# A small DRAM-to-DRAM copy issued ahead of the first loads of a rotary-embedding kernel

## The chip, the cores and the metric

The kernel runs on one core of a Trainium2 chip. The metric is the device time of one execution in microseconds (us). Several executions are timed, always beside runs of the kernel before on the same chip, and the median is given.

## The reference

```python
# x: (8, 8, 1024, 64) float32, scale = 0.5
angles = np.outer(positions * scale, freqs)          # 1024 x 32
cos, sin = np.cos(angles), np.sin(angles)
out_first  = x_first * cos - x_second * sin          # halves of the last axis
out_second = x_first * sin + x_second * cos
```

The kernel must read 16.8 MB and write 16.8 MB.

## The kernel before

x is cut into eight tiles of 128 x 4096. Tile 0 is loaded as float32 by SyncE (X0f); tiles 1 to 7 are loaded by GpSimd, cast to float16 on the way. Two small loads on ScalarE's queue bring the positions (8 KB) and the frequencies (128 B):

```python
X0f = xin.tile([P, N], FP32, name="X0f")
nc.sync.dma_start(out=X0f, in_=xv[0])

pos_i64 = consts.tile([HP, K], positions.dtype)
nc.scalar.dma_start(out=pos_i64, in_=positions.rearrange("(q k) -> q k", k=K))
freq_row = consts.tile([1, half], FP32)
nc.scalar.dma_start(out=freq_row, in_=freqs[None, :])
# ... loads of X[1] to X[7] on gpsimd ...
# two small matmuls spread frequencies and positions over the partitions,
# VectorE makes the angles (y, m, r, ra), ScalarE their sine and cosine
```

Then follow eight rounds of four VectorE instructions, a cast to float32 on ScalarE and a 2 MB store:

```python
for u in (1, 0, *range(2, NU)):
    # ps = X*sin; X = X*cos; X[first] -= ps[second]; X[second] += ps[first]   (VectorE)
    OUT = xout.tile([P, N], FP32, tag="O")
    pin(nc.scalar.copy(out=OUT, in_=X[u].rearrange("p k h j -> p (k h j)")))
    nc.sync.dma_start(out=ov[u], in_=OUT)
```

## Time and profile before

| what | value |
|---|---|
| time, median of 3 runs | 85.48 us (85.28 to 85.62) |
| span of the profiled execution | 83.9 us |
| VectorE busy | 62.6 us, 75% |
| ScalarE busy | 37.4 us, 45% |
| DMA engines | busy in nearly every slice from about 4 us on |
| bytes read and written in HBM | 16.79 and 16.78 MB |

The page gives the share of busy time of each engine, a strip of 40 slices, and the chain of work that ended last. VectorE's 75% and the DMA engines' full strip are both near a limit, so the page alone doesn't say which sets the end; the prediction takes it from the first packets of the last store. "Landing" below is the moment at which a transfer's completion semaphore has its last count. A transfer is moved in packets; what one queue has given to one DMA engine, in order, is its ring on that engine. The "head" is the part of the kernel up to the landing of the two small loads.

### The profile page before, as it was taken

How to read it: one execution, taken by the hardware profiler on the slowest of the kernel's cores; microseconds unless marked ns; L12 is line 12 of the kernel's file. 1: busy time of each engine (PE TensorE's matmuls, PEld its weight loads, DVE VectorE, ACT ScalarE, POOL GpSimd, SP SyncE). 2: the span in 40 equal slices, each digit the busy share in tenths (PEclk: the TensorE clock that was granted, in tenths of full speed). 3: DMA queues.
4: the chain of work that ended last, by engine and by line, in shares of the span. 5: the costliest groups of instructions: out<-in, count | busy, mean ns of one | idle time of the engine just before them, and what ended most of it. 6: DMA issues, size and time to landing. Idle time of an engine off the chain costs nothing.

```text
span 83.9 us, 151 instructions
## 1 busy us (share of the span) xinstructions
PE 1.1 (1%) x4; PEld 0.9 (1%) x4; DVE 62.6 (75%) x40; ACT 37.4 (45%) x12; POOL 4.5 (5%) x13
## 2 busy tenths in 40 slices
PE   0002300000000000000000000000000000000000
PEld 0002200000000000000000000000000000000000
DVE  0010699889999999999999999999999999600000
ACT  1400000799749309608905921950880591294000
POOL 5960000000000000000000000000000000000000
DMA  3599999999999999999999999999999999998890
GB/s 78 207 402 328 289 207 219 215 211 223 203 230 203 231 191 238 313 336 305 313 348 324 313 313 277 426 438 438 438 430 414 445 414 430 438 430 375 375 500 0
DMA packets 2338, 26.22 MB, mean 313 GB/s; under 512 B 274, under 2 KB 290, under 8 KB 290
## 3 DMA queue, kind: packets, MB, share of 16 engines
q1 hardware_dynamic: 1296, 18.87, 53.6%
q0 software_dynamic: 1008, 7.34, 42.7%
q10 hardware_dynamic: 34, 0.01, 0.2%
HBM read 16.79 MB, written 16.78 MB: 400 GB/s over the span
## 4 chain that ended last, share of the span: by engine, by line
DVE 72%; DMA 8%; ACT 7%; DVEq 1%; PE 1%; issue 1%; ACTq 1%
DVE X L136 22%; DVE ps L135 21%; DVE X L137 12%; DVE X L140 9%; DMA freq_row<-in_freqs_dram 8%; ACT OUT L144 4%; DVE r L116 3%; DVE y L107 3%; ACT sinT L120 2%; DVE m L114 1%; DVEq L176 1%; PE cfreq L92 1%; PE pos_ps L100 1%; ACTq L64 0%; DVE posf L104 0%
## 5 line engine op out<-in xcount | busy, mean ns | idle before, releaser
L144 ACT CAST OUT<-X 128x4096 f32<-128x4096 f16 x8 | 28.8, 3605 | 25.0 <-DVE X L140 25.0
L135 DVE TENSOR_TENSOR ps<-X,sinT 128x4096 f16<-128x4096 f16 x8 | 18.3, 2284 | 0.7 <-ACT sinT L120 0.7
L136 DVE TENSOR_TENSOR X<-X,cosT 128x4096 f16<-128x4096 f16 x8 | 18.3, 2292 | 0.3
L137 DVE TENSOR_TENSOR X<-X,ps 128x2048 f16<-128x2048 f16 x8 | 9.8, 1224 | 0.3
L140 DVE TENSOR_TENSOR X<-ps,X 128x2048 f16<-128x2048 f16 x8 | 9.7, 1217 | 0.0
L120 ACT ACTIVATE sinT<-r 128x2048 f16<-128x2048 f32 x1 | 1.9, 1910 | 12.2 <-DVE r L116 12.2
L71 POOL DMA_DIRECT2D X<-in_x_dram x7 | 3.9, 567 | 0.8 <-POOLq L162 0.8
L127 ACT CAST X<-X0f 128x4096 f16<-128x4096 f32 x1 | 3.6, 3587 | 0.0
L104 DVE COPY posf<-pos_ps 128x64 f32<-128x64 f32 x1 | 0.2, 225 | 4.0 <-PE pos_ps L100 4.0
L95 DVE CAST pos_row<-pos_i 16x64 f32<-16x64 int32 x1 | 0.2, 241 | 3.9 <-DMA pos_i<-in_positions_dram 3.9
L116 DVE SCALAR_TENSOR_TENSOR r<-m,y 128x2048 f32<-128x2048 f32 x1 | 2.3, 2292 | 0.0
L107 DVE TENSOR_TENSOR y<-posf,cfreq 128x2048 f32<-128x2048 f32 x1 | 2.3, 2286 | 0.0
L120 ACT ACT_TABLE_LOAD x1 | 1.3, 1283 | 1.7 <-issue 1.7
L126 ACT ACTIVATE cosT<-ra,quarter 128x2048 f16<-128x2048 f32 x1 | 2.0, 1985 | 0.0
L114 DVE TENSOR_SCALAR m<-y 128x2048 f32<-128x2048 f32 x1 | 1.2, 1227 | 0.0
L122 DVE TENSOR_SCALAR ra<-r 128x2048 int32<-128x2048 int32 x1 | 1.2, 1226 | 0.0
L88 DVE MEMSET coef<- 1x128 f32 x1 | 0.2, 165 | 0.8 <-PEq L162 0.8
L92 PE MATMUL cfreq<-freq_row,coef 1*128 1x32 f32 x2 | 0.6, 392 | 8.0 <-DMA freq_row<-in_freqs_dram 8.0
L100 PE MATMUL pos_ps<-pos_row,sel 16*128 16x64 f32 x2 | 0.7, 432 | 0.0
L92 PEld LDWEIGHTS cfreq<-freq_row,coef 1*128 1x128 f32 x2 | 0.5, 308 | 7.9 <-issue 7.9
L100 PEld LDWEIGHTS pos_ps<-pos_row,sel 16*128 16x128 f32 x2 | 0.5, 328 | 0.0
L77 POOL TENSOR_SCALAR_AFFINE_SELECT sel<-sel 16x128 f32<-16x128 f32 x1 | 0.3, 332 | 0.1
(6 smaller groups left out, 0.7 us busy)
## 6 DMA issues: line engine op xcount, KB each, us to landing
out_dram<-OUT SPq DMA_DIRECT2D x8, 2048.0 KB, 14.3
X<-in_x_dram POOLq DMA_DIRECT2D x7, 1024.0 KB, 24.5
X0f<-in_x_dram SPq DMA_DIRECT2D x1, 2048.0 KB, 10.2
pos_i<-in_positions_dram ACTq DMA_DIRECT2D x1, 8.0 KB, 4.1
freq_row<-in_freqs_dram ACTq DMA_DIRECT2D x1, 0.1 KB
```

The lines of the kernel that those rows point to most:

```text
L71: nc.gpsimd.dma_start(out=X[u].rearrange("p k h j -> p (k h j)"), in_=xv[u])
L100: nc.tensor.matmul(out=pos_ps, lhsT=sel.rearrange("q a b -> q (a b)"), rhs=pos_row, start=True, stop=True)
L107: pin(nc.vector.tensor_tensor(out=y, in0=posf.unsqueeze(2).broadcast_to((P, K, half)), in1=cfreq.unsqueeze(1).broadcast_to((P, K, half)), ...
L114: pin(nc.vector.tensor_scalar(out=m, in0=y, scalar1=_MAGIC, scalar2=None, op0=ALU.add))
L116: pin(nc.vector.scalar_tensor_tensor(out=r, in0=m, scalar=_MAGIC, in1=y, op0=ALU.subtract, op1=ALU.subtract))
L120: pin(nc.scalar.activation(out=sinT, in_=r, func=AF.Sin, bias=0.0, scale=-_TWO_PI_DN))
L127: pin(nc.scalar.copy(out=X[0].rearrange("p k h j -> p (k h j)"), in_=X0f))
L135: pin(nc.vector.tensor_tensor(out=ps, in0=X[u], in1=sin_b, op=ALU.mult))
L136: pin(nc.vector.tensor_tensor(out=X[u], in0=X[u], in1=cos_b, op=ALU.mult))
L137: pin(nc.vector.tensor_tensor(out=X[u][:, :, 0, :], in0=X[u][:, :, 0, :], in1=ps[:, :, 1, :], op=ALU.subtract))
L140: pin(nc.vector.tensor_tensor(out=X[u][:, :, 1, :], in0=ps[:, :, 0, :], in1=X[u][:, :, 1, :], op=ALU.add))
L144: pin(nc.scalar.copy(out=OUT, in_=X[u].rearrange("p k h j -> p (k h j)")))
```

## The change

One DMA is added, first on ScalarE's queue: sixteen rows of 128 floats (512 B), 1 MiB apart, are copied from x to out within DRAM. The result stores later overwrite all of them, so the result doesn't change. The question is what a transfer of 8 KB costs in a kernel that moves 33.6 MB.

```diff
     X0f = xin.tile([P, N], FP32, name="X0f")
     nc.sync.dma_start(out=X0f, in_=xv[0])
+
+
+    R = 16
+    xr = x.rearrange("b h s d -> (b h s d)").rearrange("(r n) -> r n", r=R)
+    outr = out.rearrange("b h s d -> (b h s d)").rearrange("(r n) -> r n", r=R)
+    nc.scalar.dma_start(out=outr[:, 0:128], in_=xr[:, 0:128])
 
     pos_i64 = consts.tile([HP, K], positions.dtype)
     nc.scalar.dma_start(out=pos_i64, in_=positions.rearrange("(q k) -> q k", k=K))
```

## The prediction

> **What bounds the kernel now.** I read the page's strip of the DMA engines first, then the chain that ended last, then the waits, then busy time by stage, and last the packet records that the trace keeps for every DMA packet (queue, start, duration, size).
>
> From the page, the busy share of the 16 DMA engines in 40 slices of 2.1 us:
>
> ```profile
> DMA  3599999999999999999999999999999999998890
> ```
>
> The engines are full from about 4 us to the end. The kernel reads 16.79 MB and writes 16.78 MB, and the last stores complete 4.9 us apart (63.00, 67.88, 72.72, 77.56 us in the semaphore updates): that is 2 MB in 4.87 us. Eight loads and eight stores at that pace are 78 us. So DMA alone nearly makes the 83.9 us, whatever the page's "DVE 72%" of the chain says.
>
> The chain, in order of time (start us, us, what):
>
> ```profile
> 0.74 0.41 ACTq L64
> 1.16 0.03 issue
> 1.19 6.64 DMA freq_row<-in_freqs_dram
> 7.82 0.14 issue
> 7.96 0.60 PE cfreq L92 x2
> 8.56 0.49 PE pos_ps L100 x2
> ...
> 15.24 1.92 ACT sinT L120
> 17.16 0.02 issue
> 17.19 2.30 DVE ps L135
> ...
> 71.59 1.15 DVEq L176
> 72.73 0.03 ACTq L144
> 72.76 0.04 issue
> 72.80 3.60 ACT OUT L144
> ```
>
> The reader is to see that the chain begins with the 128 bytes of freq_row, issued at 1.19 us and landed at 7.82 us, and that from there to 76.4 us no piece waits: angles, sine, eight rounds on VectorE (6.92 us each), the last cast. The waits say the same:
>
> ```profile
> PE cfreq L92 <- DMA freq_row<-in_freqs_dram: 8.0, 1, 8.0
> PEld cfreq L92 <- issue: 7.9, 1, 7.9
> DVE posf L104 <- PE pos_ps L100: 4.0, 1, 4.0
> DVE pos_row L95 <- DMA pos_i<-in_positions_dram: 3.9, 1, 3.9
> DVE ps L135 <- ACT sinT L120: 0.7, 1, 0.7
> ```
>
> VectorE never waits for an x tile; positions land 3 us before freq_row and don't count. Now the end, by stage (window: us, busy of PE, PEld, DVE, ACT, POOL, clock, DMA share, GB/s):
>
> ```profile
> 54.00:77.20 23.20, 0.00 (x0) 0.00 (x0) 18.52 (x12) 12.46 (x4) 0.00 (x0) 1.00 0.99 422
> 77.20:84.00 6.80, 0.00 (x0) 0.00 (x0) 0.00 (x0) 0.00 (x0) 0.00 (x0) 1.00 0.73 308
> ```
>
> The two bounds meet at 77.2 us. The DMA engines finish the last-but-one store between 76.74 and 77.22 us (its completion packets). The last store is issued at 76.45 us and its first packets start at 77.27 to 77.41 us on all engines alike, the ones free since 76.74 and the one free at 77.22. So it is its issue that they waited for (0.82 us from issue to first packet), not the engines. The compute chain therefore ends last, by 0.05 us against the last engine. That has a one-sided consequence: a later head of the chain moves the end by its full amount; an earlier head would gain next to nothing.
>
> **What the Trainium skill says.** Three places in its page "DMA: Bandwidth & Descriptors" bear on the change.
> (1) "Queues, rings and completion order": each DMA engine round-robins between the queues with work, a packet at a time, and works off one queue's ring in order. The trace agrees. I followed each engine's packets by end and start. Leaving out two engines' muddled first microseconds, all go: x (X0f, 16 KB, 0.62 us), pos data (25 ns when undisturbed), x, pos completion, x, x, x, then x and gpsimd-load packets alternately. The engine that carries freq_row has: pos data 3.34, pos completion 4.39, three x packets at 4.39, 5.01, 5.62, freq data 6.25, a load packet 6.25, x 6.86, freq completion 7.48, landed 7.82.
> (2) "Why a DMA increments its semaphore by 16 and not by 1": the slowest dimension sets the number of engines, the lowest-numbered ones being used. By that the new copy (16 rows on both sides) and positions use all 16 and freq_row one. The trace agrees for the old two: 16 packets for positions, one for freq_row, and freq_row's semaphore moves at 1.79 and 7.82 us.
> (3) "Latency and other measured facts" puts HBM access at 0.2 us on average and 2 us under high load. The trace has more in a full queue: the first store, issued at 27.93 us among loads, has its first packets at 31.94 to 33.3 us, 4.0 us and more, against 0.82 us for the last store on idle engines. So a packet entering a busy engine stands behind some 3.2 us or more of packets already taken, about five of 0.62 us. That also explains freq_row: three x packets got in between it and positions because it came a little later.
>
> **The change, part by part.** Nothing is removed and no compute instruction is added or moved: the instruction orders of both kernels on TensorE, VectorE, GpSimd and SyncE are the same. ScalarE's queue gets one DMA ahead of positions and freq_row.
> - Bytes: 16 rows of 512 B, one data and one completion packet on each engine: about 25 + 9 ns per engine by positions' packets of the same size. Nothing in 80 us.
> - ScalarE issue: positions took 0.41 us from 0.74. The copy takes that place, so positions go from about 1.16 and freq_row from about 1.6 us, some 0.45 us later. ScalarE itself is not needed before 15.24 us.
> - The dependency that the overwriting makes: the built kernel's first store has an extra wait for the copy's semaphore. That store is issued at 27.93 us, the copy should land by some 5 to 6 us. Worth 0. The semaphores shift by one among the eight; each reused one belongs to a transfer long landed. Worth 0.
> - Ring order: this is the cost. The copy's packets take positions' early places (data about 3.5, completion about 4.3 us). Positions are now issued when freq_row was (1.16 against 1.19 us), so they should get its place: data near 6.2 us. From there each further packet of ScalarE's queue waits a full round, one x packet and one load packet, 1.24 us (6.245 to 7.480 in the records). On the freq engine: pos data 6.25, pos completion 7.48, freq data 8.72, freq completion 9.95, landed 10.3 us. X0f's completion packets come at about 10 to 10.5 us, so the round keeps its length that long.
> - Sum: freq_row lands at about 10.3 instead of 7.82 us: +2.5 us, the whole of it on the path, for the chain is tight behind it and the last store has 0.05 us of slack. 85.48 + 2.5 = 87.95 us. Because the sizes below 2.5 have more weight than those above, I put the prediction at 87.7.
>
> **The rivals.**
> - One place fewer: positions are issued 0.1 us sooner than freq_row was (their issue is shorter, 0.41 against 0.53 us), and may get in before the three x packets. Then pos data would come about 5.0, completion 5.6 to 6.2, freq data 7.5, completion 8.7: +1.24 us, 86.7 us, 1.5%, within 2%. For it: the exact filling of the engines in the first 2 us is not visible. Against: freq_row missed those places by three packets, not by one.
> - The issue alone counts, +0.45 us, 85.9 us, or the copy takes a first-use cost on itself (positions' first packets took up to 0.44 us against 0.025) and the others keep their times. Against: freq_row's 6.6 us lie in waiting behind packets, and the ring is in order.
> - Worse: a DRAM-to-DRAM copy may hold the ring longer than a load, since its completion waits for a write to DRAM, or positions and freq_row each find the engines full anew (1.9 us between positions' completion and freq data). Each lost place is 1.24 us: +3.7 us, 89.2 us. No DRAM-to-DRAM transfer is in this trace to say.
> - The copy delays the first store, or is hidden since DMA is the bound anyway: both give 85.5. The first is excluded by 20 us of slack; the second by the 0.05 us of slack in the last store. DMA being full in the middle doesn't help, for its backlog is used up exactly when the last store is issued.
> - Faster: nothing is removed, and before the last store there is no slack to win on the DMA side. 2%.
>
> **Range and chances.** Delay 0 to 0.6 us: 12%; about 1.2: 20%; 1.7 to 2.8: 53%; more: 15%. The line of 2% is 1.71 us. Slower by over 2%: 0.67; within: 0.31; faster: 0.02. Range for 8 in 10: 86.4 to 88.8 us.
>
> **What would show it.** In the changed profile: the DMA piece of the chain that ends with freq_row's landing near 10.3 us (right) or below 9.2 (wrong); positions landing near 7.9; every later piece of the chain with its old length and shifted by the same amount; no wait of the first store on anything but its cast; the last store's landing again about 6.2 us after its issue. The prediction is wrong if freq_row lands at its old time, if the copy lands later than positions, if VectorE shows a new wait later on, or if the end moves by less than freq_row does.

## The result, and the profile after

| kernel | time, median | range | ratio, 95% interval |
|---|---|---|---|
| before | 85.38 us | 85.12 to 85.62 (4 runs) | |
| changed | 88.97 us | 88.83 to 89.06 (4 runs) | 1.0419 (1.0383 to 1.0455) |

A ratio is the mean time of one kernel's runs over that of the other's runs of the same rounds, so it is not quite the ratio of the medians. The change costs 3.6 us. The direction was predicted, the size was not: 87.7 us was said, and 88.97 lies just above the range (86.4 to 88.8).

The start of the chain that ended last, changed kernel (start us, us, what):

```profile
0.75 0.61 ACTq L67
1.37 0.03 issue
1.40 0.60 ACTq L70
2.00 0.04 issue
2.04 9.28 DMA freq_row<-in_freqs_dram
11.31 0.14 issue
11.45 0.60 PE cfreq L98 x2
...
18.73 1.92 ACT sinT L126
...
76.28 3.60 ACT OUT L150
```

L67 is the copy, L70 the load of positions. The frequencies land at 11.31 us instead of 7.82, 3.49 us later. From there on every piece has its old length: the sine starts at 18.73 instead of 15.24 us (+3.49), the last cast at 76.28 instead of 72.80 (+3.48). The whole loss is made before 11.4 us.

The DMA issues (KB each, median us from issue to landing), positions in the kernel before, then the copy and positions in the changed one:

```profile
pos_i<-in_positions_dram ACTq DMA_DIRECT2D x1, 8.0 KB, 4.1
...
out_dram<-in_x_dram ACTq DMA_DIRECT2D x1, 8.0 KB, 7.3
pos_i<-in_positions_dram ACTq DMA_DIRECT2D x1, 8.0 KB, 9.1
```

An 8 KB copy took 7.3 us to land, and positions, which took 4.1 us before, took 9.1. The Trainium skill, "Perfetto Trace Analysis", "DMA Instruction — HWDGE (DVE, Sync)", warns that a DMA instruction that looks fast in the profile may still be waiting for its execution. The runs agree: in the kernel before, freq_row was issued in 0.53 us and landed 6.6 us after its issue began.

The end, by stage (window, us, then busy time and count of PE, PEld, DVE, ACT and POOL, clock, DMA share, GB/s):

```profile
54.00:78.50 24.50, 0.00 (x0) 0.00 (x0) 21.99 (x14) 13.04 (x4) 0.00 (x0) 1.00 0.91 387
78.50:80.70 2.20, 0.00 (x0) 0.00 (x0) 0.00 (x0) 1.38 (x1) 0.00 (x0) 1.00 0.00 0
80.70:87.40 6.70, 0.00 (x0) 0.00 (x0) 0.00 (x0) 0.00 (x0) 0.00 (x0) 1.00 0.74 313
```

Before the last store the DMA engines now stand still (share 0.00), where in the kernel before that store met them just as they came free. In the packet records they end the store ahead of it at 78.89 us and begin the last at 80.74. So in the kernel before the two bounds met, and in the changed one the compute chain alone sets the end.

Why were the frequencies 3.49 us late? These are the packets of the engine that carries freq_row, from the packet records (start in us; x is a 16 KB packet of X0f, load one of GpSimd's loads; data and done are the data and completion packets of a ScalarE DMA):

```
before:  pos data 3.34, x, pos done 4.39, x, x, x 5.62, freq data 6.25, load, x, freq done 7.48
changed: x, x, x, x, x 5.37, copy data 6.00, load, x, copy done 7.25, load, x,
         pos data 8.48, load, x, pos done 9.73, load, freq data 10.34, load, freq done 10.97
```

The copy came behind X0f's first five packets on each engine (80 of X0f's packets start ahead of it, five for each of 16). Call the place behind X0f's first packet (data near 3.4 us) the early one and the place behind its first five (near 6 us) the late one: the copy did not take the early place of positions; it took the late place of freq_row.

### The profile page after: what moved, and what is told of

The parts are those of the page before. It is cut to its first block, busy times and chain, and to the rows that moved or that the text cites.

```text
span 87.3 us, 153 instructions
## 1 busy us (share of the span) xinstructions
PE 1.1 (1%) x4; PEld 0.9 (1%) x4; DVE 62.5 (72%) x40; ACT 37.4 (43%) x12; POOL 4.5 (5%) x13
## 4 chain that ended last, share of the span: by engine, by line
DVE 69%; DMA 11%; ACT 6%; ACTq 1%; DVEq 1%; PE 1%; issue 1%
DVE X L142 21%; DVE ps L141 20%; DVE X L143 11%; DMA freq_row<-in_freqs_dram 11%; DVE X L146 9%; ACT OUT L150 4%; DVE r L122 3%; DVE y L113 3%; ACT sinT L126 2%; DVE m L120 1%; DVEq L182 1%; ACTq L67 1%; ACTq L70 1%; PE cfreq L98 1%; PE pos_ps L106 1%
## 5 line engine op out<-in xcount | busy, mean ns | idle before, releaser
L98 PE MATMUL cfreq<-freq_row,coef 1*128 1x32 f32 x2 | 0.6, 390 | 11.4 <-DMA freq_row<-in_freqs_dram 11.4
L98 PEld LDWEIGHTS cfreq<-freq_row,coef 1*128 1x128 f32 x2 | 0.5, 304 | 11.4 <-DVE pos_row L101 11.4
```

## The experiments

The theory after the result: (a) each engine takes ScalarE's packets in order, one per round, and a round lasts 1.24 us while both X0f and GpSimd's loads have packets waiting; (b) who is issued at once with X0f comes behind its first packet, who is issued some tenths later comes behind the first five (c2 below found four); (c) the copy is late by its own slower issue and loses that race, and everything behind it moves along. The main rivals: a DRAM-to-DRAM copy costs by itself wherever it stands; the distance of its rows costs; the number of DMAs alone costs; VectorE's chain is not what the end follows. Eleven kernels were run, all with correct results.

| run | what is on ScalarE's queue, or changed | freq_row landed, us | time, median us | ratio to before |
|---|---|---|---|---|
| before | pos, freq | 7.82 | 85.4 | |
| changed | copy, pos, freq | 11.31 | 88.97 | 1.042 |
| a1_copy_last | pos, freq, copy | 7.61 | 85.34 | 0.999 |
| a2_copy_second | pos, copy, freq | 9.95 | 87.71 | 1.027 |
| a3_load_first | small load, pos, freq | 10.04 | 87.62 | 1.026 |
| a4_contig | copy of adjacent rows, pos, freq | 10.61 | 88.95 | 1.040 |
| b2_sp_behind | pos, freq; copy on SyncE behind X0f | 7.47 | 85.30 | 1.000 |
| c2_late_pos | pos 0.29 us later, freq | 8.71 | 86.55 | 1.014 |
| c1_sp_first | copy, pos, freq; X0f 0.43 us later | 10.29 | 88.15 | 1.033 |
| b4_freq_sp_first | pos; freq on SyncE ahead of X0f | 1.94 | 85.73 | 1.005 |
| d1_two_copies | copy, copy, pos, freq | 12.42 | 90.25 | 1.056 |
| b1_one_row | copy of 16 x 32 B, pos, freq | 11.24 | 88.98 | 1.041 |
| b3_freq_first | freq, pos | 2.45 (pos 7.95) | 85.59 | 1.003 |

A landing is that of the profiled execution, a time is the median of all, so the two need not match within a row: the profiled execution of the kernel before took 85.65 us. Within the profiled executions, the time less the landing of freq_row is 77.74 to 77.84 us for the kernel before and for all eight kernels with a later freq_row. So the delay of freq_row passed to the end whole, in each of them.

### a1_copy_last: the copy behind the two loads

```diff
-    nc.scalar.dma_start(out=outr[:, 0:128], in_=xr[:, 0:128])   # first
     (loads of pos_i64 and freq_row on nc.scalar)
+    nc.scalar.dma_start(out=outr[:, 0:128], in_=xr[:, 0:128])
```

> The same copy, but third on ScalarE's queue, behind positions and freq_row. Theory (what costs is only that the copy stands ahead of the two small loads in one ring): positions land near 4.9 us and freq_row near 7.8 us as in the kernel before, and the time is 85.4 us, within 0.5% of it. Rival (the copy costs wherever it stands, by its write to DRAM or by the first store's extra wait for it): the time stays near 89 us, or at least over 87.

Measured: 85.34 us, ratio 0.9993 (0.9976 to 1.0009). Positions landed at 4.82 and freq_row at 7.61 us. The copy with all its bytes, its write to DRAM and the extra wait of the first store costs nothing when nothing needed soon stands behind it. The rival that it costs wherever it stands falls.

### b2_sp_behind: the copy on the other queue

```diff
-    nc.scalar.dma_start(out=outr[:, 0:128], in_=xr[:, 0:128])
+    nc.sync.dma_start(out=outr[:, 0:128], in_=xr[:, 0:128])     # behind X0f
```

> The same copy issued from SyncE, behind X0f, and ScalarE's queue as in the kernel before. Theory (the cost is the copy's place ahead of the small loads in ScalarE's ring): positions and freq_row keep their places, freq_row lands near 7.7 us, 85.4 us within 0.5%. Rival (the copy's DRAM-to-DRAM descriptors or bytes disturb the engines wherever they come from): freq_row over 9 us, 86.5 us or more.

Measured: 85.30 us, ratio 0.9997 (0.9984 to 1.001). freq_row landed at 7.47 us; the copy itself at 12.07, 10.9 us after its issue began. Nothing waits for it before the first store.

### a2_copy_second: the copy between them

```diff
     (load of pos_i64 on nc.scalar)
+    nc.scalar.dma_start(out=outr[:, 0:128], in_=xr[:, 0:128])
     (load of freq_row on nc.scalar)
```

> The copy between positions and freq_row. Theory (places in the ring, a round of 1.24 us for each packet once the engines are full): positions keep their early place and land near 4.9 us, the copy takes the place that freq_row had (data near 6.2, completion near 7.5 us), freq_row's packets follow at 8.7 and 9.95 us and land near 10.3 us, so +2.5 us, 87.9 us. Rival (a DRAM-to-DRAM copy holds the ring by itself for longer than a load of its size would): freq_row lands at 11 us or later, 88.7 us or more.

Measured: 87.71 us, ratio 1.0268 (1.0239 to 1.0298). On the engine of freq_row: copy data 5.92, copy done 7.17, freq data 8.40, freq done 9.64, landed 9.95 us. These are steps of 1.25, 1.23 and 1.24 us. A copy ahead of one load costs two rounds, no more; a copy doesn't hold the ring for longer than a load would. This kernel costs about what had been predicted for the change (87.7 us), because here something does hold the early place.

### a3_load_first: an ordinary load in the copy's place

```diff
-    nc.scalar.dma_start(out=outr[:, 0:128], in_=xr[:, 0:128])
+    rows = consts.tile([R, 128], FP32)
+    nc.scalar.dma_start(out=rows, in_=xr[:, 0:128])
```

> In place of the copy a load of the same sixteen rows of 512 B into an SBUF tile that nothing reads, first on ScalarE's queue. Theory A (a DRAM-to-DRAM copy is slower to issue, 0.61 us on ScalarE against 0.41 us for positions, and therefore comes behind the first five X0f packets): the load is issued in about 0.41 us, takes the early place between X0f's first and second packet, positions take freq_row's old place, freq_row lands near 10.3 us, 87.9 us. Theory B (it does not matter what the first DMA is; three DMAs on this queue lose the early place in any case): data of the first load near 5.7 us, freq_row lands near 11.3 us, 88.9 us.

Measured: 87.62 us, ratio 1.026 (1.0232 to 1.0289). The issues on ScalarE (start us, us):

```profile
0.74 0.41 ACTq L68 DMA_DIRECT2D rows<-in_x_dram  x1
1.18 0.44 ACTq L71 DMA_DIRECT2D pos_i<-in_positions_dram  x1
1.64 0.53 ACTq L73 DMA_DIRECT2D freq_row<-in_freqs_dram  x1
```

The same issues of the changed kernel, where the copy is L67:

```profile
0.75 0.61 ACTq L67 DMA_DIRECT2D out_dram<-in_x_dram  x1
1.40 0.60 ACTq L70 DMA_DIRECT2D pos_i<-in_positions_dram  x1
2.04 0.62 ACTq L72 DMA_DIRECT2D freq_row<-in_freqs_dram  x1
```

The load is issued in 0.41 us, the copy in 0.61, and what follows the copy is slower too. The load took the early place (it landed at 4.70 us), positions the late one (landed 7.81), and freq_row landed at 10.04 us. So the outcome is theory A's: three DMAs need not lose the early place; the first of them lost it because it was a copy. That the slower issue is the whole reason is not shown by this run (see what stays open). This load does just what the prediction said that the copy would do.

### c2_late_pos: no copy, but positions a little later

```diff
+    tc.keep_in_program_order(nc.vector.memset(pos_i64.bitcast(I32), 0))
     (load of pos_i64 on nc.scalar, now waits for the memset; freq_row behind it)
```

> No copy at all: the kernel before, with VectorE clearing the positions tile first, so that the issue of positions on ScalarE waits for it and ends some 0.2 to 0.4 us later (near 1.4 to 1.5 instead of 1.15 us); freq_row stays behind it. Theory (the early place is a race: what is issued some tenths later comes behind X0f's first five packets on each engine): positions' data near 5.8 us and landing near 7.5 us, freq_row one or two rounds of 1.24 us later than before (its data at 7 to 8.5, landing near 9 to 10.3 us), so +1.2 to +2.5 us, 86.6 to 87.9 us, from a delay of a few tenths. Rival (it is something in the DRAM-to-DRAM copy itself, not its issue time, that cost the early place): positions stay early or shift by the same tenths, freq_row lands by 8.3 us, 85.4 to 85.9 us.

Measured: 86.55 us, ratio 1.0142 (1.0127 to 1.0156). The issues on ScalarE (start us, us):

```profile
1.03 0.38 ACTq L65 DMA_DIRECT2D pos_i<-in_positions_dram  x1
1.44 0.53 ACTq L67 DMA_DIRECT2D freq_row<-in_freqs_dram  x1
```

The issue of positions began at 1.03 instead of 0.74 us, 0.29 later. Positions' data then came at 4.76 to 5.83 us, behind four X0f packets instead of one, and landed at 6.78 instead of 4.85; freq_row landed at 8.71. A delay of 0.29 us cost 1.93 us at positions and 1.2 us of time. That the places behind X0f's first packets are a race of tenths is shown, without any copy. The expectation was a little off in its numbers: positions lost three places, not four, and landed 0.7 us sooner than expected.

### c1_sp_first: the copy as in the change, X0f a little later

```diff
+    rows = consts.tile([16, 128], FP32)
+    nc.sync.dma_start(out=rows, in_=<16 x 512 B of tile 0 of x>)
     nc.sync.dma_start(out=X0f, in_=xv[0])
```

> The changed kernel, with a small load of 16 x 512 B (its tile is not read) on SyncE ahead of X0f, so that X0f is issued some 0.4 us later while the copy stays at 0.75 us. Theory (race between the copy's issue and X0f's first packets): the copy gets an early place, its data before 4 us; positions may get one too or take the place near 6 us; freq_row lands at 10.5 us or sooner, 1 us or more better than the changed kernel less the 0.4 us that X0f starts later, 87 to 88.3 us. Rival (a DRAM-to-DRAM copy needs over 4 us by itself before its data moves): its data at 5.7 us or later as before, freq_row at 11.3 us or later, 88.9 us or more.

Measured: 88.15 us, ratio 1.033 (1.0315 to 1.0345). The issues to landing (KB each, us):

```profile
out_dram<-in_x_dram ACTq DMA_DIRECT2D x1, 8.0 KB, 2.4
rows<-in_x_dram SPq DMA_DIRECT2D x1, 8.0 KB, 1.7
pos_i<-in_positions_dram ACTq DMA_DIRECT2D x1, 8.0 KB, 6.8
```

With X0f issued at 1.18 instead of 0.75 us, the same copy landed after 2.4 us instead of 7.3; its data moved before 2.8 us. So it was mostly the five packets ahead of it, and not a slowness of the copy, that made 7.3 us. Positions' data came at 6.21 to 6.58 us, and freq_row landed at 10.29 us, 1.02 us sooner than in the change; that X0f's packets start later (2.25 instead of 1.75 us) takes part of the gain. The copy also needed more time than the load of the same size that SyncE issued at the same moment: 2.4 against 1.7 us to landing, and its first data came at 2.13 against 1.76 us.

### a4_contig and b1_one_row: neither the rows nor the bytes

```diff
-    nc.scalar.dma_start(out=outr[:, 0:128], in_=xr[:, 0:128])
+    # a4: 16 rows of 512 B side by side, outr[0, 0:2048] <- xr[0, 0:2048]
+    # b1: outr[0:1, 0:128] <- xr[0:1, 0:128], which the build cuts into 16 x 32 B
```

> The copy first as in the change, but sixteen rows that lie side by side in DRAM (8 KB in one piece, still cut into 16 rows of 512 B on both sides). Theory (the spacing of the rows, 1 MiB, is not what makes the copy late): its data packets start near 5.7 us again and freq_row lands near 11.3 us, 88.9 us. Rival (the spacing of 1 MiB slows its reads or writes): the copy gets the early place, freq_row lands near 10.3 us or sooner, 87.9 us or less.

> The copy first, but of 512 B in one piece, which is cut into sixteen pieces of 32 B. Theory (it is packets and places that count, not bytes): as the changed kernel, freq_row near 11.3 us, 88.9 us within 0.6. Rival (the bytes or the sixteen distant rows count): clearly nearer to the kernel before, under 87.9 us.

Measured: a4 88.95 us, ratio 1.0398 (1.0358 to 1.0439); b1 88.98 us, ratio 1.0408 (1.0392 to 1.0425). Neither the 1 MiB between the rows nor fifteen sixteenths of the bytes matter. The profiled execution of a4 was the fastest of its four (88.36 us) and has freq_row at 10.61 us, sooner than the 11.3 expected. In it, on the engine of freq_row, one packet and not two lay between the copy's data (about 5.90 us) and its completion (6.53, against 7.25 in the changed kernel), and all that stands behind came 0.72 us sooner, freq_row's data at 9.62; the place can thus vary by a packet from one execution to the next. The medians don't differ.

### d1_two_copies: a second copy

```diff
     nc.scalar.dma_start(out=outr[:, 0:128], in_=xr[:, 0:128])
+    nc.scalar.dma_start(out=outr[:, 128:256], in_=xr[:, 128:256])
```

> Two copies first (the second of the next 128 columns of the same rows), then positions and freq_row. Theory (two rounds for each DMA ahead in the ring, 1.24 us a round while X0f's packets last, about 0.62 us when they are gone at some 10.3 us): copy data 5.7 and completion 7.0, second copy 8.2 and 9.5, positions near 10.3 to 10.8 and 10.9 to 11.4, freq_row near 11.6 and 12.2 us, landed near 12.5 us, that is +1.3 us on the changed kernel, about 90.2 us. Rival 1 (each copy has a fixed cost of its own, 3.5 us like the first): 92.4 us. Rival 2 (a fixed 2.5 us for each): 91.4 us. Rival 3 (the first copy alone costs): 89 us.

Measured: 90.25 us, ratio 1.0555 (1.0537 to 1.0573); freq_row landed at 12.42 us. The second copy costs 1.3 us, not 3.5 and not 2.5. When positions' turn comes, X0f's data packets have gone, and on the engine of freq_row the steps shrink from 1.25 us (second copy: data 8.37, done 9.62) to 0.61 (positions' data 10.23, then 10.87, 11.48, 12.09). This separates the number of rounds from their length. On ScalarE the issue of positions took 0.91 us here.

### b3_freq_first: the two loads exchanged

```diff
-    (load of pos_i64, then load of freq_row)
+    (load of freq_row, then load of pos_i64)
```

> No copy: freq_row first and positions second on ScalarE's queue. Theory (one early place, whoever is first gets it): freq_row lands before 5 us, positions take the later place, their data near 5.9 and landing near 7.5 to 8 us, and the head is as long as before: 85.4 us within 1%. Rival (freq_row is late because it is a one-engine transfer of 128 B): freq_row is still late with positions early or late, and the time 86 us or more.

Measured: 85.59 us, ratio 1.0031 (1.0012 to 1.0051). From the waits (who waited for whom: us in total, times, longest):

```profile
DVE pos_row L100 <- DMA pos_i<-in_positions_dram: 7.0, 1, 7.0
...
PE cfreq L97 <- DMA freq_row<-in_freqs_dram: 2.6, 1, 2.6
```

freq_row, whose 128 B took until 7.82 us before, landed at 2.45 us when issued first, and positions now come late (landed 7.95). One early place is to be had, and both loads are needed, so the exchange gains nothing.

### b4_freq_sp_first: an earlier head

```diff
+    nc.sync.dma_start(out=freq_row, in_=freqs[None, :])   # ahead of X0f
     nc.sync.dma_start(out=X0f, in_=xv[0])
     (load of pos_i64 alone on nc.scalar)
```

> No copy: freq_row is issued from SyncE ahead of X0f, positions alone on ScalarE. This tests the step that an earlier head gains next to nothing, since the DMA engines are the other bound. Theory: freq_row lands before 4 us, positions near 4.9 us, VectorE starts on the angles some 3 us earlier and ends 3 us earlier, but the last store waits in the queue for the stores ahead of it (over 9 us from its issue to landing instead of 6.2), and the time is 85.0 to 85.9 us, within 1% of the kernel before. Rival (the chain on VectorE is the bound): 82.3 to 83 us.

Measured: 85.73 us, ratio 1.0047 (1.0035 to 1.006). Both small loads landed by 2.3 us. VectorE's longest wait is now one for a tile of x, and the last cast starts earlier. From the waits, and from the chain (start us, us, what):

```profile
DVE ps L140 <- DMA X<-in_x_dram: 2.9, 1, 2.9
```

```profile
69.64 3.60 ACT OUT L149
```

The last cast starts 3.16 us sooner than before (72.80), and the time is not shorter but 0.4 us longer. X0f's first packet came at 2.12 instead of 1.77 us, behind freq_row, which fits that loss but is not tested alone. The last store was issued at 73.27 us and landed at 83.00, 9.7 us later instead of 6.2: its first packets started at 76.86 us, when those of the store ahead of it ended (76.81 to 77.43). So a later head loses time here, and an earlier one wins none. No version here beats the kernel before.

## Why the prediction was right or wrong

**The bound and its slack: right.** The head's delay was to pass to the end in full, because the last store had only 0.05 us to spare. The head moved by 3.49 us, the last cast by 3.48, the median by 3.59. (The last store's issue began at 76.43, not 76.45 us, so its first packets came after 0.84 us; with idle engines, in the changed kernel, after 0.83. It did wait for its issue.) The one-sidedness, which was only argued from packet times, is shown by b4_freq_sp_first.

**What costs nothing: right.** The bytes (a1, b2, b1), the extra wait of the first store and the shift of the semaphores (a1 has both, and no change). The copy landed at 8.10 us, later than the 5 to 6 us that were expected, but the first store is issued only at 31.42.

**Ring order and the round of 1.24 us: right.** In the changed kernel the copy's completion, positions' data and positions' completion follow at 1.25, 1.23 and 1.25 us on the engine of freq_row. Only the length of the last two steps was misjudged: it was said that the round keeps its length until about 10 to 10.5 us; in fact it was short from 9.73 us on, 0.61 and 0.63 us, as X0f had no data packets left.

**The step that failed** is the first of the ring-order paragraph: "The copy's packets take positions' early places (data about 3.5, completion about 4.3 us)." They took the late place, data at 5.66 to 6.49 us and completion at 6.67 to 7.74. The prediction's own estimate that a packet entering a busy engine stands behind about five others was the right depth; wrong was that the copy would enter before those five were taken. (Its comparison with the access time of HBM did not bear on this: the 4.0 us of the first store are waiting in a queue.) The assumption under the step, that the copy is issued like positions in 0.41 us, failed too: 0.61 us. Hence the next step, that positions "should get its place: data near 6.2 us", was wrong in turn; they came at 7.90 to 8.97. The sum had two rounds (2.48 us) and got four steps behind the copy's completion, of 1.23, 1.25, 0.61 and 0.63 us, 3.72 in all, from which 0.23 goes off since the copy came 0.23 to 0.25 us before freq_row's old place: 3.49. Experiment a3 shows the predicted course with a load instead of a copy, and a2 with the copy behind a load; both came out at 87.6 to 87.7 us. That it was a race is shown from both sides: positions issued 0.29 us later lost three of their places (c2), and the copy won its early place when X0f came 0.43 us later (c1).

The prediction had named a slower copy as a rival ("Worse", 89.2 us) and gave it 15%, for want of any DRAM-to-DRAM transfer in the trace. That 89.2 is near the 88.97 measured is no credit to it, for neither mechanism it gave is what happened. The ring is not held by the copy's completion: a2 shows ordinary rounds behind a copy, and in c1, on engines not yet busy, the copy's completion follows its data by 0.02 us. And positions and freq_row did not each find the engines full anew: they followed the copy at the steps given above.

**What stays open.** Why the issue of a DRAM-to-DRAM copy takes 0.57 to 0.61 us wherever it stands, and why positions behind it take 0.60 us (0.91 behind two) instead of 0.41 to 0.44, isn't settled. How much of the copy's lateness is this issue can be read from two runs in which nothing but small transfers had reached the engines: in b4 positions' first data came at 1.74 us, 1.00 us after the start of their issue and 0.63 after its end; in c1 the copy's came at 2.13 us, 1.38 us after the start and 0.80 after the end. So a copy is some 0.39 us behind a load issued at the same moment, 0.22 of it by the longer issue (0.59 against 0.37 us) and 0.17 after it; X0f's first packets come at 1.75 us. This fits c2: there positions ended their issue at 1.41 us, later than the copy's 1.37 in the change, and yet came behind four packets, the copy behind five; with 0.63 and 0.80 us added, an estimate puts them at the engines at 2.04 and 2.17 us. What the 0.17 us are is open, and no run has a load whose issue is as long as a copy's.

## What to carry to other kernels

A tiny transfer is not judged by its bytes but by what stands behind it in the same queue and ahead of it on the engines: here 8 KB put ahead of a small load cost about 2.3 us, two rounds (a2, a3), 3.6 us where the early place was lost as well (the change), and nothing when they were put behind. Issue the small loads that the first computation waits for ahead of anything in their queue that isn't needed soon. Against a large transfer on another queue they run a race: 0.29 us decided whether positions came behind one large packet or behind four (c2). And when two bounds meet at the end, as here, a change at the head can lose time and not win any: in b4 both small loads landed by 2.3 us, and the time did not fall.

## What the Trainium skill lacked or had wrong

- The Trainium skill's "DMA: Bandwidth & Descriptors", "Issuing engines are not separate DMA queues", says that initiating DMAs on multiple engines "will only save the time on the sequencer it takes to initiate the DMA, which is usually small relative to the DMA itself". Here the same copy cost 3.6 us at the front of ScalarE's queue (88.97 us), and nothing at its end (85.34) or behind X0f on SyncE's (85.30). What stands behind a DMA in its queue is missing from that statement; the ring order itself stands in the page's section "Queues, rings and completion order".
- The same page's "Queues, rings and completion order" has the round-robin by packet, which the traces confirm, but not how many packets an engine has already taken when a new queue comes in. Here it was four (c2) or five (the change) of 16 KB, 0.62 us each, for what is issued together with X0f or 0.3 us after it and reaches the engines later; the first store needed 4.0 us from issue to first packet on busy engines, against 0.83 us on idle ones (the changed kernel's last store, 79.91 to 80.74 us).
- The same page, "Latency and other measured facts", has rates of large copies between HBM tensors, but no figure for how long the issue and the landing of a small DRAM-to-DRAM copy take beside those of a load. Here it is 0.57 to 0.61 us of issue against 0.41 us for a load of the same size, and 2.4 us against 1.7 us to landing with both at the head of their queues.
